# A forgetting-attention and gMLP trunk in split fp32: the input projection's first two column blocks by turns

## The chip, the cores and the metric

The kernel runs on one core of one Trainium2 chip. The metric is device time in microseconds (us), 2053.89 as the median of three runs (2053.75 to 2054.33). Engines are named as in the profile: TensorE is PE (its weight loads PEld), VectorE is DVE, ScalarE is ACT, GpSimd is POOL, and SyncE's queue (SP) issues most transfers.

## The reference

Two layers act on a residual stream of 256 tokens by 2048 channels, in float32. Layer 0 mixes tokens with forgetting attention, layer 1 with a gated MLP over chunks; each is followed by a squared-ReLU MLP. The change lies in the first layer's attention:

```python
h = rmsnorm(x, g_mix[i])
proj = h @ w_in                      # q, k, v (3 x 2048 columns) and 16 gate columns
q = rmsnorm(q, g_q) * HEAD_DIM ** -0.5 ; k = rmsnorm(k, g_k)      # per head of 128
c = cumsum(log_sigmoid(f_logit + b_f))                            # per token and head
s = q @ k.T + (c[t] - c[s]), causal;  o = softmax(s) @ v;  x = x + o @ w_out
x = x + squared_relu(rmsnorm(x, g_mlp[i]) @ w1) @ w2
```

## The kernel before

Every weight is used as two parts, since a product of float32 numbers is made of three on PE: ACT casts a weight to its high part (`split_hi`, L79), DVE subtracts it for the low part (`split_lo`, L87), and PE adds high x high, high x low and low x high (L150 to L152). Weights come in halves of 128 x 1024 numbers (512 KB), called weights below: two blocks of 128 rows by 512 columns each. One **step** is what PE does with one such weight: 2 row blocks x 2 halves of the tokens x 3 products = 12 matmuls of 128 x 512. A column block (512 columns of q, k or v for four heads) takes 8 steps and sums in two PSUM banks (`acc`, one per 128 tokens; four banks in all, so two column blocks at a time). The input projection has 12 column blocks, in the order q, k, v of heads 0 to 3, then q, k, v of heads 4 to 7, and so on; steps 0 to 7 are the first block, 8 to 15 the second.

x transposed lies in DRAM and comes into one buffer (`xT`, named A in the profile) in 8 pieces of 256 KB, two row blocks each. `h_init` scales a piece and splits it in two parts, `H` (ACT L199, DVE L200), and H is then used by every column block.

`run` writes the order of the work by hand. In step i it asks for the weights that are listed for it, splits ahead (low part of step i + 3, high part of step i + 4), issues PE's matmuls, and then the tasks that were put on that step with `at(step, fn)`. All engines take their work in this order. There are 4 buffers for weights, so that the weight of step n + 4 is asked for when the low part of step n has been made; 5 for high parts, 4 for low parts; and two PSUM banks for short use (`aux`).

The tasks around the start are these, with their steps before. `x_norm` (2) asks SP for x itself, 2 MB, and has its squares summed on ACT in step 8 and made into the factor `r_mix` on POOL. `fox_f` (3) asks for the gate's weights, splits them (7), multiplies them with H (9, 16 matmuls) and turns the result to tokens (11); `fox_f_gate` (12) makes the log of the gate and `fox_c` (14) sums it over tokens. `fox_qk` squares a finished q or k block on ACT (L422), takes a power on POOL (L176), one step later scales it on DVE, which frees its accumulator banks (L431), and three steps later transposes it on PE through `aux` (L441). For the first block it is put 3 steps after its last step, 10, for the second at its last step, 15. `fox_bias` (15) fetches the decay rows back from DRAM, `fox_mask` (18) adds the mask; scores come in steps 23 and 24, their transposes in 28 and 29, the outputs in 30 and 31. The second group of heads has its q block done in step 31 and transposed in 34.

## Time and profile before

| | |
|---|---|
| median of three runs | 2053.89 us |
| the profiled execution | 2054.6 us, of which the span is 2052.9 us |
| PE busy | 2045.1 us, 12628 matmul instructions |
| DVE, ACT, POOL busy | 1730.5, 1202.8, 114.4 us |
| HBM read over the span | 430.63 MB, 211 GB/s |

Times inside the profile count from the start of the span. A matmul's busy time is longer than the distance to the next one, as matmuls are pipelined: distances between starts tell whether PE waited. Two instructions in one row, as in "x2", carry their common time.

### The profile page before, as it was taken

To read this page: it belongs to the slowest core of one execution; us is meant where nothing else is said; L and a number is where in the kernel's file an instruction comes from. 1 tells how busy PE (TensorE), PEld (TensorE's weight loads), DVE (VectorE), ACT (ScalarE), POOL (GpSimd) and SP (SyncE) were. 2 spreads that over 40 slices of the span, in tenths; PEclk is the share of its full clock that TensorE was granted. 3 is DMA by queue.
4 is the path that set the end of the run, shared out by engine and by line. 5 is a ranking of instruction groups with operands and counts; after the bars stand their busy time and mean duration, and the time that the engine had idled before them with its cause. 6 is when DMAs were issued, how large, how long until landed. Compare 5 with 4: busy or idle time off the path is not lost.

```text
span 2052.9 us, 32611 instructions
## 1 busy us (share of the span) xinstructions
PE 2045.1 (100%) x12628; PEld 1820.8 (89%) x12628; DVE 1730.5 (84%) x2078; ACT 1202.8 (59%) x1607; POOL 114.4 (6%) x112
## 2 busy tenths in 40 slices
PE   9999999999999999999999999999999999999999
PEld 6888888899999999999988999889999999999997
DVE  5656867779999999999997577768999999999998
ACT  6555555555665656665566455455656556565664
POOL 1110111000000000000000000000000000000000
PEclk9999999999999999999999999999999999999999
DMA  7456666477788877887865567757788777887785
GB/s 278 167 187 209 198 208 204 150 251 226 236 265 270 244 231 234 266 268 232 243 219 190 200 232 212 214 179 235 243 277 249 229 240 257 274 243 228 237 266 166
DMA packets 118602, 469.99 MB, mean 229 GB/s; under 512 B 11808, under 2 KB 30128, under 8 KB 95152
## 3 DMA queue, kind: packets, MB, share of 16 engines
q1 hardware_dynamic: 104352, 395.49, 52.8%
q0 software_dynamic: 13952, 72.37, 19.0%
q8 instruction: 99, 1.62, 0.3%
q14 instruction: 55, 0.45, 0.1%
q10 hardware_dynamic: 144, 0.06, 0.0%
HBM read 430.63 MB, written 2.11 MB: 211 GB/s over the span
## 4 chain that ended last, share of the span: by engine, by line
PE 99%; DMA 1%; ACT 0%; DVE 0%; SPq 0%; issue 0%; DVEq 0%
PE Q L700 14%; PE acc L574 13%; PE acc L575 13%; PE acc L576 13%; PE R L700 10%; PE acc L700 8%; PE acc L150 7%; PE acc L151 7%; PE acc L152 7%; PE acc L763 2%; DMA w_stage<-in_fox_in 1%; PE aux L237 1%; PE aux L899 0%; PE aux L441 0%; PE aux L470 0%; PE aux L519 0%
## 5 line engine op out<-in xcount | busy, mean ns | idle before, releaser
L79 ACT CAST w_hi<-b 128x1024 fp32r<-128x1024 f32 x469 | 486.1, 1048 | 282.7 <-DVE b L729 154.3
L574 PE MATMUL acc<-H,w_hi 128*128 128x256 f32 x2304 | 649.3, 282 | 0.0
L576 PE MATMUL acc<-H,w_lo 128*128 128x256 f32 x2304 | 646.9, 281 | 0.0
L575 PE MATMUL acc<-H,w_hi 128*128 128x256 f32 x2304 | 646.7, 281 | 0.0
L87 DVE TENSOR_TENSOR w_lo<-w_stage,w_hi 128x1024 fp32r<-128x1024 f32 (+1 forms) x470 | 573.0, 1225 | 80.2 <-ACT w_hi L79 38.5
L79 ACT CAST w_hi<-w_stage 128x1024 fp32r<-128x1024 f32 (+1 forms) x470 | 488.6, 1047 | 243.7 <-PE acc L152 80.0
L87 DVE TENSOR_TENSOR w_lo<-b,w_hi 128x1024 fp32r<-128x1024 f32 x469 | 564.5, 1223 | 44.7 <-issue 34.8
L575 PEld LDWEIGHTS acc<-H,w_hi 128*128 128x128 f32 x2304 | 434.1, 188 | 10.4
L574 PEld LDWEIGHTS acc<-H,w_hi 128*128 128x128 f32 x2304 | 433.3, 188 | 10.6
L576 PEld LDWEIGHTS acc<-H,w_lo 128*128 128x128 f32 x2304 | 433.9, 188 | 0.0
L150 PE MATMUL acc<-w_hi,H 128*128 128x512 f32 x512 | 206.4, 403 | 0.4 <-ACT w_hi L79 0.4
L151 PE MATMUL acc<-w_lo,H 128*128 128x512 f32 x512 | 203.4, 397 | 1.4 <-DVE w_lo L87 0.9
L152 PE MATMUL acc<-w_hi,H 128*128 128x512 f32 x512 | 202.9, 396 | 0.0
L700 PE MATMUL Q<-w_hi,SC 128*128 128x512 f32 (+1 forms) x592 | 192.3, 374 | 0.0
L729 DVE TENSOR_TENSOR b<-b,b 128x2048 f32<-128x2048 f32 (+1 forms) x74 | 154.0, 2082 | 0.2
L700 PEld LDWEIGHTS Q<-w_hi,SC 128*128 128x128 f32 x592 | 108.4, 188 | 18.4
L151 PEld LDWEIGHTS acc<-w_lo,H 128*128 128x128 f32 x512 | 96.6, 189 | 24.1 <-DVE w_lo L87 3.1
L152 PEld LDWEIGHTS acc<-w_hi,H 128*128 128x128 f32 x512 | 96.4, 188 | 23.4
L150 PEld LDWEIGHTS acc<-w_hi,H 128*128 128x128 f32 x512 | 96.6, 189 | 22.7 <-ACT w_hi L79 1.2
L700 PE MATMUL Q<-w_lo,SC 128*128 128x512 f32 (+1 forms) x296 | 110.3, 373 | 0.0
L612 ACT ACTIVATE m_a<-m_a 128x512 f32<-128x512 f32 x64 | 40.6, 635 | 114.8 <-DVE m_a L606 113.1
L700 PE MATMUL R<-w_hi,SC 128*128 128x512 f32 (+1 forms) x352 | 107.4, 359 | 0.0
(173 smaller groups left out, 2521.4 us busy)
## 6 DMA issues: line engine op xcount, KB each, us to landing
w_stage<-in_w SPq DMA_DIRECT2D x272, 512.0 KB, 6.5
b<-in_w SPq DMA_DIRECT2D x120, 1024.0 KB, 7.2
w_stage<-in_fox_in SPq DMA_DIRECT2D x94, 512.0 KB, 4.4
b<-in_w POOLq DMA_DIRECT2D x30, 1024.0 KB, 10.6
b<-b POOLq DMA_DIRECT2D x30, 1024.0 KB, 9.2
w_stage<-in_sgu_v SPq DMA_DIRECT2D x32, 512.0 KB, 3.7
w_stage<-in_sgu_u SPq DMA_DIRECT2D x32, 512.0 KB, 5.5
w_stage<-in_sgu_out SPq DMA_DIRECT2D x20, 512.0 KB, 3.9
```

Source lines behind the costliest of these rows:

```text
L79: self.nc.scalar.copy(out=hi[:, sl], in_=self.staged[i][:, sl])
L87: self.nc.vector.tensor_tensor(out=lo[:, sl], in0=st[:, sl], in1=hi[:, sl].bitcast(F32), op=ALU.subtract)
L150: nc.tensor.matmul(out=acc[t], lhsT=xh, rhs=hi[:, ws], start=(kb == k_first), stop=False)
L151: nc.tensor.matmul(out=acc[t], lhsT=xh, rhs=lo[:, ws], start=False, stop=False)
L152: nc.tensor.matmul(out=acc[t], lhsT=xl, rhs=hi[:, ws], start=False, stop=(kb == KB - 1))
L574: nc.tensor.matmul(out=acc[c], lhsT=hi[:, ws], rhs=xh, start=(kb == 0), stop=False)
L575: nc.tensor.matmul(out=acc[c], lhsT=hi[:, ws], rhs=xl, start=False, stop=False)
L576: nc.tensor.matmul(out=acc[c], lhsT=lo[:, ws], rhs=xh, start=False, stop=(kb == KB - 1))
L612: nc.scalar.activation(out=a, in_=a, func=AF.Square)
L700: nc.tensor.matmul(out=bank[bname], lhsT=s, rhs=w[:, ws], start=(before == k == m == 0), stop=(k == 3 and m == 2), skip_group_check=True)
L729: return lambda: nc.vector.tensor_tensor(out=quad[o], in0=quad[x], in1=quad[y], op=op)
L763: nc.tensor.matmul(out=acc[t], lhsT=s, rhs=w[:, ws], start=(q == h == k == m == 0), stop=(q == h == k == 1 and m == 2))
```

## The change

The first two column blocks, q and k of heads 0 to 3, no longer come one after the other but by turns: steps 0, 2, .. 14 are the first block's weights, 1, 3, .. 15 the second's. Each piece of x transposed is then used in two steps. Its transfer is asked for just ahead of the weight of the same step (`load_x`), every second step, where before all eight pieces were asked for at the outset; `h_init` scales it in every second step. The tasks move: `x_norm` to 5 with its squares in 10, `fox_f` to 9 (split 13, product 15, by token 17), the gate to 18, its sums to 21. `fox_qk` of the first block runs in 14, right at its end, that of the second in 20, 5 steps after its end; the decay rows come in 23, the mask in 25, the scores in 27 and 28, their transposes in 32 and 33, the outputs in 34 and 35. From the third block on weights, steps and their tasks stand as before.

```diff
+    def load_x(self, i):
+        if i % 2 == 0 and i < KB:
+            sl = slice(i * S, (i + 2) * S)
+            self.nc.sync.dma_start(out=self.xT[:, sl], in_=self.ins["xT"][:, sl])
+
     def h_init(self, i):
-        for k in (2 * i, 2 * i + 1):
-            self.put_scaled(self.xT[:, k * S:(k + 1) * S], C_GMIX0, k)
+        if i % 2 == 0 and i < KB:
+            for k in (i, i + 1):
+                self.put_scaled(self.xT[:, k * S:(k + 1) * S], C_GMIX0, k)
...
+        two = [self.unit_steps([ins["fox_in"][u * 4 + c] for c in range(4)], "H", done) for u, done in enumerate((
+            lambda acc, step: self.fox_qk(0, 0, acc, step),
+            lambda acc, step: self.at(step + 5, lambda: self.fox_qk(0, 1, acc, step + 5))))]
+        for _ in range(KB // 2):
+            for w in range(2):
+                next(two[w], None)
+                last[0, w] = self.steps - 1
         for g in range(4):
             for w in range(3):
                 u = g * 3 + w
+                if u < 2:
+                    continue
...
-                if u == 0:
-                    last[g, w] = self.unit_x(src, "H", lambda acc, step, done=done: self.at(
-                        step + 3, lambda: done(acc, step + 3)))
-                else:
-                    last[g, w] = self.unit_x(src, "H", done)
-            s = last[g, 1] + (8 if g == 0 else 5)
-            self.at(last[g, 1] + 3, self.fox_mask)
+                last[g, w] = self.unit_x(src, "H", done)
+            s = last[g, 1] + (12 if g == 0 else 5)
+            self.at(last[g, 1] + (10 if g == 0 else 3), self.fox_mask)
...
-        self.at(2, self.x_norm)
-        self.at(9, self.alloc_a)
-        self.at(3, self.fox_f)
-        self.at(12, self.fox_f_gate)
-        self.at(14, self.fox_c)
+        self.at(5, self.x_norm)
+        self.at(KB, self.alloc_a)
+        self.at(9, self.fox_f)
+        self.at(18, self.fox_f_gate)
+        self.at(21, self.fox_c)
...
-        self.at(8, stats)
+        self.at(10, stats)
...
-            self.at(step + (5 if g == 0 else 4), lambda: self.fox_bias(g))
+            self.at(step + (9 if g == 0 else 4), lambda: self.fox_bias(g))
...
-                for i in range(KB // 2):
-                    sl = slice(2 * i * S, 2 * (i + 1) * S)
-                    nc.sync.dma_start(out=xT[:, sl], in_=ins["xT"][:, sl])
-                    if i < STAGE_BUFS:
-                        self.load(i)
+                for i in range(STAGE_BUFS):
+                    self.load_x(i)
+                    self.load(i)
...
                     for j in self.loads.get(i, ()):
+                        self.load_x(j)
                         self.load(j)
-                    if i + SPLIT_AHEAD < KB // 2:
-                        self.h_init(i + SPLIT_AHEAD)
+                    self.h_init(i + SPLIT_AHEAD)
```

SP's queue from the first transfer on, before: A is x transposed, w_stage a weight (the first two in two pieces of 128 x 512), x_res is x.

```order
L990 DMA A<-in_xT 128x512
L65 DMA w_stage<-in_fox_in 128x512 x2
L990 DMA A<-in_xT 128x512
L65 DMA w_stage<-in_fox_in 128x512 x2
L990 DMA A<-in_xT 128x512
L65 DMA w_stage<-in_fox_in 128x1024
L990 DMA A<-in_xT 128x512
L65 DMA w_stage<-in_fox_in 128x1024
L990 DMA A<-in_xT 128x512 x4
L65 DMA w_stage<-in_fox_in 128x1024 x5
L315 DMA x_res<-in_x 128x2048 x2
```

The same place now, from the second transfer on (the first is a piece of x transposed, as before) up to x:

```order
L65 DMA w_stage<-in_fox_in 128x512 x4
L193 DMA A<-in_xT 128x512
L65 DMA w_stage<-in_fox_in 128x1024 x2
L193 DMA A<-in_xT 128x512
L65 DMA w_stage<-in_fox_in 128x1024 x2
L193 DMA A<-in_xT 128x512
L65 DMA w_stage<-in_fox_in 128x1024 x2
L193 DMA A<-in_xT 128x512
L65 DMA w_stage<-in_fox_in 128x1024 x2
L193 DMA A<-in_xT 128x512
L65 DMA w_stage<-in_fox_in 128x1024 x2
L327 DMA x_res<-in_x 128x2048 x2
```

Six pieces of x transposed now stand among twelve weights, and x behind the twelfth weight and not behind the ninth.

PE where the gate's product with H (L342 before, L354 now) stands between two steps, with the waits for other engines, before (steps 9 and 10):

```order
L152 MATMUL acc<-w_hi,H 128x512
L342 MATMUL aux<-H,tt_266 32x512 [waits DVE_49]
L342 MATMUL aux<-H,tt_266 32x512 x15
L150 MATMUL acc<-w_hi,H 128x512
L151 MATMUL acc<-w_lo,H 128x512
L152 MATMUL acc<-w_hi,H 128x512
L150 MATMUL acc<-w_hi,H 128x512
```

and now (steps 15 and 16):

```order
L152 MATMUL acc<-w_hi,H 128x512
L354 MATMUL aux<-H,tt_376 32x512 [waits DVE_49]
L354 MATMUL aux<-H,tt_376 32x512 x15
L150 MATMUL acc<-w_hi,H 128x512 [waits DVE_49,PE_49,Activation_49]
L151 MATMUL acc<-w_lo,H 128x512
L152 MATMUL acc<-w_hi,H 128x512
L150 MATMUL acc<-w_hi,H 128x512 [waits DVE_49,Activation_49]
```

The product has moved to the place where the third block opens its two accumulator banks, each with a wait for DVE.

PE where the first block's q is transposed (L441 before, L453 now), before, at the end of step 13:

```order
L152 MATMUL acc<-w_hi,H 128x512
L441 MATMUL aux<-ident,qk_n 128x128 [waits DVE_49,Activation_49] x2
L441 MATMUL aux<-ident,qk_n 128x128
L441 MATMUL aux<-ident,qk_n 128x128 [waits Activation_49]
L441 MATMUL aux<-ident,qk_n 128x128 [waits DVE_49]
L441 MATMUL aux<-ident,qk_n 128x128 [waits Activation_49]
L441 MATMUL aux<-ident,qk_n 128x128
L441 MATMUL aux<-ident,qk_n 128x128 [waits Activation_49]
L150 MATMUL acc<-w_hi,H 128x512
```

and now, at the end of step 17, with the gate's product by token (L363) ahead of it:

```order
L152 MATMUL acc<-w_hi,H 128x512
L363 MATMUL aux<-sel,probsT 128x16 [waits Activation_49]
L363 MATMUL aux<-sel,probsT 128x16 x3
L453 MATMUL aux<-ident,qk_n 128x128 [waits Pool_49]
L453 MATMUL aux<-ident,qk_n 128x128 x3
L453 MATMUL aux<-ident,qk_n 128x128 [waits Activation_49]
L453 MATMUL aux<-ident,qk_n 128x128 x3
L150 MATMUL acc<-w_hi,H 128x512
```

The fifth transpose opens the second bank of the pair; it waited for DVE before and waits for ACT now.

## Rows read from the trace of the kernel before

**Rows 1.** The page, busy time by engine: us (share of the span) x instructions.

```profile
PE 2045.1 (100%) x12628; PEld 1820.8 (89%) x12628; DVE 1730.5 (84%) x2078; ACT 1202.8 (59%) x1607; POOL 114.4 (6%) x112
```

**Rows 2.** PE's waits over the whole run: who waited for whom, us in total, times, longest.

```profile
PE acc L151 <- DVE w_lo L87: 0.9, 1, 0.9
PE acc L151 <- DVE gq L1010: 0.4, 1, 0.4
```

**Rows 3.** The chain that ended last, from 0 to 40 us: start, us, what.

```profile
9.01 8.70 DMA w_stage<-in_fox_in
17.74 1.05 ACT w_hi L79
...
20.03 1.23 DVE w_lo L87
```

**Rows 4.** PE's timeline: start, us, engine, line, operation; the first matmul of step 1 (10.62), 2 (13.42), 3 (16.84) and 4 (20.00) and what follows, and the gate's products behind step 9.

```profile
8.93 0.63 PE L151 MATMUL acc<-w_lo,H 128*128 128x512 f32 x1
9.36 0.63 PE L152 MATMUL acc<-w_hi,H 128*128 128x512 f32 x1
...
10.62 0.40 PE L150 MATMUL acc<-w_hi,H 128*128 128x512 f32 x1
...
13.42 0.39 PE L150 MATMUL acc<-w_hi,H 128*128 128x512 f32 x1
14.16 0.50 PE L151 MATMUL acc<-w_lo,H 128*128 128x512 f32 x1 [0.35 <-DVE gq L1010]
14.50 0.39 PE L152 MATMUL acc<-w_hi,H 128*128 128x512 f32 x1
...
16.84 0.40 PE L150 MATMUL acc<-w_hi,H 128*128 128x512 f32 x1
17.33 0.50 PE L151 MATMUL acc<-w_lo,H 128*128 128x512 f32 x1
...
20.00 0.39 PE L150 MATMUL acc<-w_hi,H 128*128 128x512 f32 x1
21.31 0.50 PE L151 MATMUL acc<-w_lo,H 128*128 128x512 f32 x1 [0.92 <-DVE w_lo L87]
...
37.97 3.86 PE L342 MATMUL aux<-H,tt 128*32 128x512 f32 x16
41.66 0.39 PE L150 MATMUL acc<-w_hi,H 128*128 128x512 f32 x1
```

**Rows 5.** DVE's timeline: the low parts of the weights of step 0 (two pieces) and step 2.

```profile
5.46 1.33 DVE L87 TENSOR_TENSOR w_lo<-w_stage,w_hi 128x512 fp32r<-128x512 f32 x2
...
12.88 1.22 DVE L87 TENSOR_TENSOR w_lo<-w_stage,w_hi 128x1024 fp32r<-128x1024 f32 x1 [2.62 <-ACT w_hi L79]
```

**Rows 6.** Windows on PE: stretch, its length, PE busy (matmuls), granted clock, share of the transfer engines, GB/s.

```profile
5.00:10.00 5.00, 4.55 (x11) 1.00 0.98 302
10.00:22.00 12.00, 10.64 (x43) 1.00 0.83 322
```

**Rows 7.** Timelines of SP, ACT and DVE: the first weight asked for behind x, its cast and its low part.

```profile
23.24 0.33 SPq L65 DMA_DIRECT2D w_stage<-in_fox_in  x1
...
32.26 1.05 ACT L79 CAST w_hi<-w_stage 128x1024 fp32r<-128x1024 f32 x1 [6.47 <-DMA w_stage<-in_fox_in]
...
33.34 1.23 DVE L87 TENSOR_TENSOR w_lo<-w_stage,w_hi 128x1024 fp32r<-128x1024 f32 x1 [5.17 <-ACT w_hi L79]
```

**Rows 8.** Timelines of PE, ACT, DVE and POOL: the second column block from its last matmul into the first bank (step 15) through the first of its eight squares, the scaled sum, the power and the scaling, to what DVE does next.

```profile
61.12 0.39 PE L152 MATMUL acc<-w_hi,H 128*128 128x512 f32 x1
...
61.61 0.37 ACT L422 ACTIVATE qk_n<-acc,r_mix 128x128 f32<-128x128 f32 x1 [2.42 <-PE acc L152]
...
64.55 0.17 DVE L175 TENSOR_SCALAR r_qk_v<-ss_qk 128x8 f32<-128x8 f32 x1 [3.75 <-ACT qk_n L422]
...
64.87 2.50 POOL L176 TENSOR_TENSOR r_qk<-r_qk_v,mhalf 128x8 f32<-128x8 f32 x1 [4.19 <-DVE r_qk_v L175]
...
67.41 1.41 DVE L431 SCALAR_TENSOR_TENSOR qk_n<-acc,r_mix,r_qk 128x512 f32<-128x512 f32 x2 [1.56 <-POOL r_qk L176]
68.74 2.35 DVE L87 TENSOR_TENSOR w_lo<-w_stage,w_hi 128x1024 fp32r<-128x1024 f32 x2
```

**Rows 9.** Timelines of PE and ACT: the eight transposes of a q block and the two copies of them.

```profile
122.67 1.03 PE L441 MATMUL aux<-ident,qk_n 128*128 128x128 f32 x8
123.31 1.27 ACT L445 ACTIVATE qT<-aux,gq 128x512 f32<-128x512 f32 x2 [2.20 <-PE aux L441]
```

**Rows 10.** Timelines of PE and ACT: the first and last output products of two heads, and the cast of them.

```profile
108.86 0.59 PE L519 MATMUL aux<-probsT,v_nat 128*128 128x256 f32 x2
...
109.94 0.38 PE L521 MATMUL aux<-probsT,v_nat 128*128 128x128 f32 x2
...
110.36 0.59 ACT L204 CAST A<-aux 128x512 fp32r<-128x512 f32 x1 [2.63 <-PE aux L521]
```

**Rows 11.** The instructions that read x (x_res), from 0 to 50 us: count, duration in ns (least, median, most), first and last start.

```profile
L181 ACT ACTIVATE m_a<-x_res x8: 614/614/623, 37.4 to 41.7; 128x512 f32<-128x512 f32 x8
```

**Rows 12.** POOL's timeline of the mask, with its wait for the decay rows, and, from the view of the decay rows in DRAM (one transfer there, four back), the times to landing.

```profile
72.36 1.29 POOL L410 TENSOR_TENSOR tt<-cb,tri 128x512 f32<-128x512 f32 x1 [4.43 <-DMA cb<-c_dram]
73.62 2.27 POOL L411 TENSOR_TENSOR cb<-cb,tri 128x512 f32<-128x512 f32 x1
...
DMA to landing us min/median/max: 3.1/4.8/10.3
```

More of the change, by code (lines that the diff above doesn't have):

```diff
@@ L1004, in run @@
                 for i in range(STAGE_BUFS, LOAD_AHEAD):
+                    self.load_x(i)
                     self.load(i)
```

## The prediction

> **What bounds the kernel now.** I read the page first. TensorE (PE) is busy 2045.1 of 2052.9 us [rows 1], so a change that leaves PE's instructions as they are can move the time only by PE's idle time, and 7.8 us is all there is in the whole span. Next came PE's waits over the whole run: the two releasers of the first 22 us that carry weight are the low part of a weight (0.9 us) and the small `gq` step that stands for it (0.4 us) [rows 2]. The chain that ended last, from 0 to 40 us, tells what is behind them: 8.70 us of a weight transfer asked for at 9.01, then the cast at 17.74, and the subtraction at 20.03 [rows 3]. So the start is bound by the arrival of weights, and from about 22 us on PE is.
>
> How much the start costs is read from when matmuls start, since a busy PE hides short gaps. One step is 12 matmuls; step 1 starts at 10.62 and step 2 at 13.42, so a step without a gap is 2.80 us, 0.233 per matmul [rows 4]. From 10.62 to the products of the forget gate at 37.97 lie steps 1 to 9: 9 x 2.80 = 25.20 if nothing waited, 27.35 as it was. The 2.15 us that were lost are all visible: 13.42 to 14.16 (0.51 too long), 16.84 to 17.33 (0.26), 20.00 to 21.31 (1.08), each followed by one start that comes 0.11 late, as at 14.16 to 14.50 [rows 4]: 0.51 + 0.26 + 1.08 + 3 x 0.11 = 2.18. These are steps 2, 3 and 4, each at its second matmul, the first that reads the low part.
>
> **What the change takes away.** PE has the same instructions in another order, so its own work costs the same. The weights of steps 2, 3 and 4 have fewer bytes ahead of them on SyncE's queue. Up to and with the weight of step 2: before, 3 blocks of x transposed and 3 weights, 2.25 MB; now 2 and 3, 2.0 MB. Step 3: 3.0 against 2.5 MB. Step 4: 4.5 against 3.25 MB. In this stretch the queue moves 302 to 322 GB/s [rows 6], which is 0.8, 1.6 and about 4 us earlier. Needed are 0.45 for step 2 (its low part starts at 12.88, takes 1.22, so ends at 14.10, and the second matmul wants it at 13.65) [rows 4, 5], 0.26 for step 3, 1.08 for step 4. The weight of step 4 also waits for its buffer, which is the first weight's; that one's low part is done at 5.46 + 1.33 = 6.8 [rows 5], so it can be asked for 2.2 us before the 9.01 of rows 3. After that the need falls: two steps take 2 weights and 1 block, 1.25 MB in 5.6 us, or 234 GB/s, under what the queue moves. All three gaps should close. Bounds: 0, if the weights land no earlier, and -2.18; I take -2.18, because the tightest, step 2, has 0.8 where 0.45 is needed.
>
> **What is moved and costs nothing.** x (2 MB) is asked for behind the weight of step 11 and no longer behind that of step 8. What stands behind it on the queue now is the weight of step 12. Before, the weight asked for at 23.24, just behind x, was cast at 32.26 after 6.47 us of waiting, and its low part was ready at 34.57 for step 9 at about 35.2, with 0.6 to spare [rows 7]. With the same 9 us, step 12's lands near 32 and is wanted at 10.62 + 11 x 2.80 = 41.4. The squares of x, 8 of 0.61 us on ScalarE [rows 11], stand in step 10 and not 8, the first user of their result in step 14; ScalarE is through with them near 42 and with the casts behind them by 48, and step 14 ends at 49.8. If that cover went, ScalarE's lateness would be paid in full at the next point. The decay rows go to DRAM in step 21 and come back for the mask; ahead of that the gap was six steps and is now four. One such transfer lands 3.1 us after its issue at the least, the way back waited 4.4 us, and the mask takes 1.29 + 2.27 us [rows 12]: about 12 us from the end of step 21 (77 us by my count) gives 90; the scores of step 27 come near 95. Nothing.
>
> **What it adds: the first block's banks.** Both column blocks now hold the four accumulator banks until step 15, and step 16 opens the third block in the first one's banks. The order of PE between steps 15 and 16 (shown with the change) has two L150 that wait for VectorE: that is the scaling by the norm, which frees the two banks. Behind them stand all further matmuls. How long that takes is in the trace at step 15 of before, the same work on the second block: its first bank is whole with the matmul at 61.12, the squares run from 61.61, the sum is scaled at 64.55, GpSimd's power takes 2.50 from 64.87, and the scaling is done between 67.41 and 68.74 [rows 8]. The matmul at 61.12 is the tenth of its step, so the step ends at 61.12 + 4 x 0.233 = 62.05: first bank free 6.0 us after it (half of 1.41 after 67.41), the second 6.7. Cover: step 15 (2.80) and the 16 products between (41.66 - 37.97 = 3.69 [rows 4]) make 6.49, and the second bank is wanted 0.70 later. It just fits, with 0.4 us. Bounds: 0, and some 4.9 us if all the squares of x [rows 11] still stood ahead on ScalarE; I take 0, the nearer.
>
> **What it adds: two waits for a small bank.** There are two auxiliary banks. In step 17 the gate's product by token and the transposes of q now stand together, and the gate is read in step 18 only. In PE's order at the end of step 17 (shown with the change) the fifth transpose waits for ScalarE, as the gate's values keep one bank and the second four transposes must take the bank of the first four. In the kernel before the product by token stood two steps ahead of them. The price is in the transposes of 122.67: ScalarE's copy starts 0.64 after the first transpose, two copies take 1.27 [rows 9], so the bank is free at 0.64 + 0.64 = 1.28, and PE would want it after 4 transposes, at 1.03 / 8 x 4 less overlap, or 0.4. That is a wait of 0.9. The same kind comes in step 34: the attention output of the first heads is put 4 steps later, from step 30 to 34, where the transposes of the next q block stand. Output and transposes need three banks. The output products start at 108.86, the last at 109.94, and ScalarE's cast of them at 110.36 [rows 10]; a cast is about 0.5, then the copy of the first transposes 0.64: free 2.65 us after 108.86, wanted at 1.22 + 0.40 = 1.62. That is 1.05. Bounds for both together: 0 (another bank is free after all) to 2.8 (VectorE's part of the output is waited for each time); I take 0.9 + 1.05 = 1.95.
>
> **Sum.** -2.18 + 0 + 0 + 1.95 = -0.23 us, on the profiled execution's own 2054.6 us (its span and 1.7 around it). That execution is 0.7 above the median of the runs, 2053.89; on the median it makes 2053.7 us.
>
> **A rule against the start.** The first step's matmuls start 0.43 us apart (8.93 to 9.36) and from 10.62 on 0.233 [rows 4]; 0.43 for 512 columns is the 1.2 GHz level, though the granted clock reads 1.00 from 5 us on [rows 6]. The change puts nothing other there. The Trainium skill (TensorE: Matmul & The Clock Gate, The HAM clock gate) says that the unit which grants the clock runs freely, and so the rise does not come at a fixed matmul of a kernel. By that rule the time could move by itself; the three times of before lie within 0.6 us, which speaks against much of it. It is the last rival below.
>
> **Rivals.**
> 1. The gaps close and the two bank waits cost nothing, as ScalarE may be quicker or another bank free: -2.18, 2051.7. For it: the copies are short. Against it: the wait on ScalarE stands in the order.
> 2. The gaps stay: the weights land no earlier because all transfers share the queue's time, and only the new waits are seen: 2053.9 + 1.95 = 2055.8. For it: the queue moved 302 to 322 GB/s while PE waited [rows 6]. Against it: 1.25 MB fewer are ahead of step 4's weight.
> 3. Slower: the first block's banks in step 16. From 0.4 us of lateness on, each further us on ScalarE, VectorE or GpSimd is paid by PE. With the squares of x in the way, 4.9 - 0.4 = 4.5: 2053.7 + 4.5 = 2058.2.
> 4. The rise of the clock falls elsewhere: ten matmuls of the first step at 0.43 instead of 0.233 are 2.0 us, so 2051.7 or 2055.7.
>
> **How the numbers follow.** Forecast 62%, own range 2052.9 to 2054.7 (half a us on either term); rival 1 12%, rival 2 10%, rival 3 11% (half of it small, 1 to 2 us), rival 4 5%. The range reaches over rival 1 and 2 and the small part of 3: 2051.4 to 2056.4. A change of 0.2%, 4.1 us, is about what a measurement of this kernel can tell from none. Faster by that is out of reach of the 2.18 us the start can give; it is left 3%. Slower by it needs the larger part of rival 3 or a wait that I have not seen: 6%. The rest, 91%, is no change.
>
> **What would show it.** In the profile of the changed kernel: from step 1 on to the products (now ahead of step 16) starts lie 0.233 apart, 15 x 2.80 = 42.0 us, so the products start near 52.6. No low part is waited for by the second matmul of steps 2 to 4. After the products L150 follows in 3.7 us; more is rival 3. In steps 17 and 34 the four transposes and the next four lie about 1.3 us apart at their starts and not 0.4. Wrong would be any PE wait beyond these before 130 us, or a first block of weights that lands as late as before.

## The result and the profile after

| | before | changed |
|---|---|---|
| median, 17 runs each | 2053.81 us (2053.47 to 2054.50) | 2057.91 us (2056.14 to 2061.58) |
| profiled execution, its span | 2054.6, 2052.9 us | 2057.55, 2055.8 us |

The ratio is 1.0021, 95% interval 1.0014 to 1.0028: the changed kernel is slower, by 4.1 us, and 1.5 us above the forecast range. The page's first part, against [rows 1]:

```profile
PE 2044.5 (99%) x12628; PEld 1820.5 (89%) x12628; DVE 1729.6 (84%) x2078; ACT 1203.2 (59%) x1607; POOL 114.3 (6%) x112
```

PE did the same work in 0.6 us less busy time, so the 2.9 us that the span grew are idle time. PE's waits over the whole run, against [rows 2] (us in total, times, longest):

```profile
PE acc L150 <- DVE qk_n L443: 2.4, 1, 2.4
PE aux L453 <- ACT qT L457: 1.6, 2, 0.8
...
PE acc L151 <- DVE w_lo L87: 0.6, 2, 0.3
```

The two waits of the start are nearly gone. One new wait of 2.4 us stands at the top: the scaling of q, which frees the first block's banks. The second row is the two expected waits for a small bank. These are idle times; by the distances between starts, used from here on, the first is 2.53 us and the second 2.04. PE's timeline of that place, against [rows 4]:

```profile
8.98 0.40 PE L150 MATMUL acc<-w_hi,H 128*128 128x512 f32 x1
...
45.38 0.39 PE L150 MATMUL acc<-w_hi,H 128*128 128x512 f32 x1
46.09 0.50 PE L151 MATMUL acc<-w_lo,H 128*128 128x512 f32 x1 [0.33 <-DVE w_lo L87]
...
51.56 3.86 PE L354 MATMUL aux<-H,tt 128*32 128x512 f32 x16
57.78 0.47 PE L150 MATMUL acc<-w_hi,H 128*128 128x512 f32 x1 [2.37 <-DVE qk_n L443]
...
59.06 0.63 PE L152 MATMUL acc<-w_hi,H 128*128 128x512 f32 x1
59.49 0.63 PE L150 MATMUL acc<-w_hi,H 128*128 128x512 f32 x1
...
62.05 0.55 PE L150 MATMUL acc<-w_hi,H 128*128 128x512 f32 x1
62.43 0.40 PE L151 MATMUL acc<-w_lo,H 128*128 128x512 f32 x1
```

Step 1 starts at 8.98, step 14 at 45.38, the gate's products at 51.56. In step 14 the second and third matmul come 0.59 later than at 0.233 a start, for a late low part. The products want 3.69 us [rows 4], so step 16 could have begun at 55.25; it began at 57.78, 2.53 late. Then, from 59.06 on, the starts lie 0.43 apart, the 1.2 GHz level, and come back to 0.233 at 62.43. The windows on PE show the fall in the granted clock too (columns as in [rows 6]):

```profile
60.00:62.00 2.00, 2.00 (x6) 0.50 0.65 213
62.00:64.00 2.00, 2.00 (x9) 0.91 0.12 49
```

Added over its matmuls, that stretch costs 1.57 us. The chain that ended last, from 28 to 58 us, leads back from the late bank (columns as in [rows 3]):

```profile
28.73 8.76 DMA w_stage<-in_fox_in
37.59 1.05 ACT w_hi L79
...
46.10 3.93 DMA w_stage<-in_fox_in
51.08 1.78 ACT qk_n L434 x10
54.27 2.60 POOL r_qk L176
56.89 0.76 DVE qk_n L443
57.78 0.47 PE acc L150
```

The squares of q began at 51.08. What stood ahead of them is in the timelines of ScalarE, which answers to the cast of [rows 7] and the squares of [rows 11], and of VectorE:

```profile
34.40 1.05 ACT L79 CAST w_hi<-w_stage 128x1024 fp32r<-128x1024 f32 x1 [5.87 <-PE acc L152]
...
37.59 1.05 ACT L79 CAST w_hi<-w_stage 128x1024 fp32r<-128x1024 f32 x1 [0.39 <-DMA w_stage<-in_fox_in]
38.55 0.63 ACT L181 ACTIVATE m_a<-x_res 128x512 f32<-128x512 f32 x1
...
43.47 0.89 ACT L206 ACTIVATE H<-A,par 128x256 fp32r<-128x256 f32 x2
44.26 2.93 ACT L79 CAST w_hi<-w_stage 128x1024 fp32r<-128x1024 f32 x3
...
50.13 1.05 ACT L79 CAST w_hi<-w_stage 128x1024 fp32r<-128x1024 f32 x1 [2.63 <-DMA w_stage<-in_fox_in]
51.08 0.36 ACT L434 ACTIVATE qk_n<-acc,r_mix 128x128 f32<-128x128 f32 x1
```

```profile
43.59 0.16 DVE L186 TENSOR_REDUCE tot_mix<-ss_mix 128x2 f32<-128x8 f32 x1 [4.55 <-ACT m_a L181]
...
43.99 0.91 DVE L207 SCALAR_TENSOR_TENSOR H<-A,par,H 128x256 fp32r<-128x256 f32 x2
44.83 3.48 DVE L87 TENSOR_TENSOR w_lo<-w_stage,w_hi 128x1024 fp32r<-128x1024 f32 x3
```

The first row names PE, but PE had long been done with that buffer; it is the weight of step 12, asked for at 24.47 behind x's 2 MB, that came late. ScalarE stood idle from 28.5 to 34.4 for it, and from then to 47.5 for 0.39 us only. The squares of x ran from 38.55 to 43.5, the last pieces of H stood behind them, and behind H, on VectorE, the low part of step 14, the first of the three from 44.83 on. That low part frees the buffer of the weight of step 18: asked for at 46.10, landed at 50.0, cast at 50.13. That cast stands in ScalarE's order ahead of the squares of q, which by the pattern of [rows 8] would have begun 0.44 us before the end of step 14, at 48.76 (51.56 less a step) - 0.44 = 48.32. They came 2.76 late. Of this the forecast's 0.4 us of margin is covered, and 2.36 are paid; from the squares to step 16 it then took 6.70 us, about 0.2 more than [rows 8] gave, which makes up the wait of 2.53.

An account of the profiles in the same way tells where the time went. "Start" is the products' start against 54.77, which is the 37.97 of before and six steps more (where they follow step 14, 51.97); "stretch" what matmuls at the 1.2 GHz level behind a stop cost; "small banks" what the transposes of steps 17 and 34 wait.

| us against before | start | wait at step 16 | stretch | small banks | sum | span, measured |
|---|---|---|---|---|---|---|
| changed | -3.21 | 2.53 | 1.57 | 2.04 | +2.93 | +2.9 |
| again | -2.15 | 2.49 | 1.66 | 2.04 | +4.04 | +4.0 |
| stats7 | -2.30 | 0 | 0 | 2.05 | -0.25 | -0.3 |
| x_spread | -3.49 | 2.45 | 0 | 2.04 | +1.00 | +0.9 |
| nopause | -3.18 | 2.49 | 0 | 0 | -0.69 | -0.6 |
| lockstep | -1.71 | 0 | 0 | 0 | -1.71 | -1.7 |
| mended2 | -2.47 | 0 | 0 | 0 | -2.47 | -2.5 |

The names are those of the experiments below. Four terms make up every span of the table to 0.1 us.

How often the stretch comes is told by the granted clock that each execution reports, to three places. In the 15 profiled executions it reads 0.999 in the six that show a stretch behind a stop and 1.000 in the nine that show none. Of the changed kernel's 17 executions the five fastest read 1.000 (2056.14 to 2057.35 us), the next nine 0.999 (2057.55 to 2059.69) and the three slowest 0.998 (2060.17 to 2061.58). By this reading most of its spread goes with the clock, and most executions had a stretch, some more than one. The reading is rounded: 4 of 85 executions of the kernel before, timed beside the experiments, read 0.999 too and lie among the rest (2053.54 to 2054.39).

### The profile page after: what moved, and what is told of

The parts are those of the page before. It is cut to its first block, busy times and chain, and to the rows that moved or that the text cites. A ratio compares the mean times of both kernels' runs of the same rounds, so it can differ in the third digit from the quotient of the medians.

```text
span 2055.8 us, 32606 instructions
## 1 busy us (share of the span) xinstructions
PE 2044.5 (99%) x12628; PEld 1820.5 (89%) x12628; DVE 1729.6 (84%) x2078; ACT 1203.2 (59%) x1607; POOL 114.3 (6%) x112
## 4 chain that ended last, share of the span: by engine, by line
PE 98%; DMA 1%; ACT 1%; issue 0%; POOL 0%; DVE 0%; DVEq 0%; ACTq 0%; SPq 0%
PE Q L712 14%; PE acc L586 13%; PE acc L587 13%; PE acc L588 13%; PE R L712 10%; PE acc L712 8%; PE acc L150 7%; PE acc L151 7%; PE acc L152 7%; PE acc L775 2%; DMA w_stage<-in_fox_in 1%; PE aux L244 1%; PE aux L453 0%; PE aux L911 0%; PE aux L482 0%; PE aux L531 0%
```

## The experiments

The theory was the chain above: ScalarE, late by the squares of x, holds the bank. The rivals were that the landing of the weights behind x does it, whatever ScalarE has to do, that the sum of the squares on VectorE does it, and that much of the loss is the clock's and not the wait's. A run without an interval is one execution beside the kernel before.

**again.** The changed kernel as it is, to see what repeats.

> The changed kernel once more, nothing edited. Theory A (a chain on ScalarE makes PE wait ahead of step 16, and the clock falls after that wait): the wait between the gate's products and step 16 is there again, 2 to 3 us beyond the products' own 3.7 us, and matmuls behind it start 0.43 us apart for a while, but the length of that stretch and of the slow one at the start (0 to 12 matmuls) may differ, since the runs spread over 5.4 us. Rival B (the wait is chance, as a late transfer): the wait changes by more than 1 us or is gone.

2058.57 us. The wait at step 16 came again, 2.49, and so did the small banks; step 1 started 1.5 us later, at 10.49. The stretch at 1.2 GHz was not behind step 16 but behind the pause in step 17, from 67.41 to 70.8:

```profile
67.00 0.66 PE L453 MATMUL aux<-ident,qk_n 128*128 128x128 f32 x4 [0.78 <-ACT qT L457]
67.41 0.58 PE L150 MATMUL acc<-w_hi,H 128*128 128x512 f32 x1
67.79 0.63 PE L151 MATMUL acc<-w_lo,H 128*128 128x512 f32 x1
68.22 0.63 PE L152 MATMUL acc<-w_hi,H 128*128 128x512 f32 x1
```

The wait came again at its full length; the place of the stretch and the start changed.

**stats7.** The squares of x three steps earlier.

```diff
-        self.at(10, stats)
+        self.at(7, stats)
```

> Only edit: the squares of x run in step 7 and no longer in step 10. Theory A1 (the squares stand in step 10 behind a cast that waits for its weight, so all that ScalarE does later is late by their 4.9 us, down to the squares of the first block's q): they fill ScalarE's idle time of 28.5 to 34.4 us, the weight of step 18 is asked for some 4 us earlier than 46.1, the first square of q starts within 0.5 us of the last matmul that it needs and no longer 2.8 us late, the wait ahead of step 16 is under 0.5 us, the clock doesn't fall there: 2053 to 2054.5 us against 2057.9. Rival A2 (the power, the sum and the scaling of the first block take too long by themselves): the wait stays at 2 us or more, 2057 us.

2053.65 us (2052.85 to 2055.15), ratio 0.9999 (0.9990 to 1.0009). ScalarE and PE in its timelines:

```profile
30.45 0.63 ACT L181 ACTIVATE m_a<-x_res 128x512 f32<-128x512 f32 x1 [1.36 <-DMA x_res<-in_x]
...
35.50 1.04 ACT L79 CAST w_hi<-w_stage 128x1024 fp32r<-128x1024 f32 x1
...
47.35 1.05 ACT L79 CAST w_hi<-w_stage 128x1024 fp32r<-128x1024 f32 x1 [0.43 <-DMA w_stage<-in_fox_in]
...
49.22 0.37 ACT L434 ACTIVATE qk_n<-acc,r_mix 128x128 f32<-128x128 f32 x1 [0.82 <-PE acc L152]
```

```profile
52.47 3.85 PE L354 MATMUL aux<-H,tt 128*32 128x512 f32 x16
56.16 0.40 PE L150 MATMUL acc<-w_hi,H 128*128 128x512 f32 x1
```

The squares run as soon as x has landed, in the time in which ScalarE had stood idle for the weight; the weight of step 18 was asked for at 42.18 instead of 46.10 and cast at 47.35; the squares of q now wait for PE; step 16 follows the products in 3.69. The weight of step 12 was cast at 35.50, no earlier than in the changed kernel (34.40), so its late landing does not by itself hold the bank. One number moved, and the kernel does what was forecast for the change, with the two small banks still there.

**x_spread.** x in four pieces of 512 KB, each behind the weight of a step, so that no weight has 2 MB ahead of it.

```diff
-        self.at(5, self.x_norm)
+        self.at(4, self.x_norm)
...
-        for t in range(NT):
-            nc.sync.dma_start(out=self.x[:, t, :], in_=self.ins["x"][:, t * D:(t + 1) * D])
...
+        part(0)
+        for j in range(1, 4):
+            self.at(self.now + j, lambda j=j: part(j))
```

> Only edit: x is asked for in four pieces of 512 KB behind the weights of steps 10, 11, 12 and 13 and no longer in two of 1 MB behind that of step 11; the squares stay in step 10. Theory A1: ScalarE is late because the weights of steps 12 to 14 arrive late behind x (cast of step 12's at 34.4 when its turn was 28.6). With smaller pieces between them that weight is cast by 32, the squares begin 1 to 3 us earlier than 38.55, and the wait ahead of step 16 falls by as much, from 2.5 to about 0 to 1.5: 2054 to 2057 us. If the total of the transfers is the limit and not their order, the weight of step 14 lands as late as before and nothing is gained: 2057.9.

2056.75 us (2055.49 to 2059.97), ratio 1.0017 (1.0007 to 1.0026). The late landing of step 12's weight is gone (cast at 31.47), and the wait at step 16 is not (2.45):

```profile
31.47 1.05 ACT L79 CAST w_hi<-w_stage 128x1024 fp32r<-128x1024 f32 x1 [2.10 <-PE acc L151]
...
37.30 1.05 ACT L79 CAST w_hi<-w_stage 128x1024 fp32r<-128x1024 f32 x1 [2.21 <-PE acc L152]
38.26 0.63 ACT L181 ACTIVATE m_a<-x_res 128x512 f32<-128x512 f32 x1
```

The squares stand in line behind step 14's cast, and start at 38.26 as against 38.55. The second row names PE, but by its starts PE was done with step 9, whose high part had that buffer, at 34.3: what came late is the weight, asked for at 28.39, where the changed kernel asked at 28.73 and cast at 37.59. So this edit moved the late landing from step 12's weight to step 14's, as the second half of the expectation had it, and does not tell what an early landing of all weights would give. With the squares where they are, asking for x in pieces does not help.

**sum_late.** Only the sum of the squares, on VectorE and GpSimd, two steps later.

```diff
-            self.total_rsqrt(ss, "mix0")
+            self.at(12, lambda: self.total_rsqrt(ss, "mix0"))
```

> Only edit: the sum of x's squares and its power are put into step 12 and no longer right behind the squares in step 10. Theory A1a (VectorE is held by that sum, so that the low part of step 14's weight is late, its buffer free late, and the weight of step 18 asked for late): VectorE goes on by 38 us, the weight of step 18 is asked for 4 us earlier, the wait ahead of step 16 is gone. Theory A1b (the low part of step 14 stands behind the scaling of x transposed's last piece, which stands behind the squares on ScalarE itself): the low part still starts near 44.8, the wait stays within 0.3 us of the 2.5 us.

2057.32 us, with a wait of 2.56. The low part of step 14 started at 44.59 and not 44.83. VectorE's sum is not what held it by more than that 0.24. What is left ahead of it on VectorE is its share of H, which waited for ScalarE.

**half.** Four squares of x instead of eight (this leaves half of the numbers out of the norm's sum).

```diff
-                for n in range(4):
+                for n in range(2):
...
-            self.total_rsqrt(ss, "mix0")
+            self.total_rsqrt(ss[:, :, 0:2], "mix0")
```

> Leaves out half of x's squares (4 of 8, so the norm's factor is too large); all else, and their place in step 10, as in the changed kernel. Theory A1 (ScalarE has no idle time from 34.4 to 47.5 us, and what is put into that stretch is paid behind it): 4 x 0.615 = 2.46 us less there, the weight of step 18 is asked for 2.4 us earlier, the squares of q start 2.4 us earlier, the wait ahead of step 16 falls from 2.5 to 0 to 0.3 us. Rival A3 (the place of the squares matters and not their length, as they hold VectorE or the weights' queue): the wait stays above 1.5 us.

2053.64 us. The wait fell from 2.53 to 0.67; the 0 to 0.3 expected left out that the products would start 0.50 earlier too, at 51.06, as step 14 no longer waits for its low part. Step 18's weight was asked for at 43.59 instead of 46.10, cast at 47.77, and the squares of q ran at once behind it:

```profile
47.77 1.05 ACT L79 CAST w_hi<-w_stage 128x1024 fp32r<-128x1024 f32 x1 [2.77 <-PE acc L152]
48.73 0.36 ACT L434 ACTIVATE qk_n<-acc,r_mix 128x128 f32<-128x128 f32 x1
```

Taking 2.4 us of squares off ScalarE brought the request forward by 2.5 and the squares of q by 2.35. Each link of the chain moved by that amount.

**stats8.** The squares of x in step 8.

```diff
-        self.at(10, stats)
+        self.at(8, stats)
```

> Only edit: the squares of x in step 8 and not in step 10. In that order they still stand behind the cast of step 12's weight, for which ScalarE waits until 34.4. Theory A1: the same work in the same full stretch in another order, so the wait ahead of step 16 stays at 2.0 to 2.6 us, and the casts of steps 13 and 14 come later, with a gap of some tenths in those steps. Rival (each step earlier helps by a step's share): two thirds of what step 7 gave, wait under 1 us.

2058.35 us. The wait ahead of step 16 went (0.06), and the loss came 15 us earlier, in steps 12 and 13:

```profile
40.98 0.39 PE L152 MATMUL acc<-w_hi,H 128*128 128x512 f32 x1
41.83 0.49 PE L150 MATMUL acc<-w_hi,H 128*128 128x512 f32 x1 [0.46 <-ACT H L206]
...
43.89 0.80 PE L151 MATMUL acc<-w_lo,H 128*128 128x512 f32 x1 [1.56 <-DVE w_lo L87]
44.48 0.63 PE L152 MATMUL acc<-w_hi,H 128*128 128x512 f32 x1
```

0.62, 1.83 and 0.36 longer than 0.233, 2.8 in all, and a stretch at 1.2 GHz behind them, of 1.2 more. This is one execution. I had expected a smaller loss at the old place. In step 8 the squares stand behind the cast of the late weight (35.42) and ahead of the H of step 12, which came at 41.29 and which PE waits for in the second row. So what counts is not earlier or later: in step 7 they stand ahead of the late weight's cast, in ScalarE's idle time.

**nopause.** The forget gate one step earlier (8, 17, 19) and the next tasks two, so that no two of these stand in steps 17 and 34 together; the squares of x stay in step 10.

```diff
-            s = last[g, 1] + (12 if g == 0 else 5)
-            self.at(last[g, 1] + (10 if g == 0 else 3), self.fox_mask)
+            s = last[g, 1] + (10 if g == 0 else 5)
+            self.at(last[g, 1] + (8 if g == 0 else 3), self.fox_mask)
...
-        self.at(9, self.fox_f)
-        self.at(18, self.fox_f_gate)
-        self.at(21, self.fox_c)
+        self.at(8, self.fox_f)
+        self.at(17, self.fox_f_gate)
+        self.at(19, self.fox_c)
...
-            self.at(step + (9 if g == 0 else 4), lambda: self.fox_bias(g))
+            self.at(step + (7 if g == 0 else 4), lambda: self.fox_bias(g))
```

> The kernel mended, but with the squares of x in step 10 as in the changed kernel: the wait ahead of step 16 is there, the two bank waits of steps 17 and 34 are not. Theory A1: the wait ahead of step 16 is 2.3 to 2.6 us (now right ahead of step 16, as the gate's products stand a step earlier). Under C1 the clock still falls behind it in some runs: 2054.5 to 2056.5, spread over 3 us. Under C2 most of the falls are gone with the pause in step 17: 2053.8 to 2054.8, spread under 2.5 us. The kernel with the squares in step 7 has 2052.5, so what lies above that is the wait and what the clock does behind it.

2054.95 us (2053.01 to 2057.36), ratio 1.0006 (0.9996 to 1.0016). The wait is still there, between 55.06 and 57.78 (2.49), the transposes wait no more, and the profile has no stretch at 1.2 GHz. But of the ten executions the five slowest, from 2055.41 on, read a granted clock of 0.999, and the five others, the profiled one among them, 1.000. By that reading the clock falls in half of the executions though step 17 has no pause, as theory C1 had it.

**mended.** Both edits: the squares in step 7 as in stats7, and the tasks as in nopause.

```diff
-        self.at(10, stats)
+        self.at(7, stats)
...
-        self.at(9, self.fox_f)
+        self.at(8, self.fox_f)
```

> The changed kernel with the squares of x in step 7, and the two waits for a small bank taken out: the gate's products in step 14, by token in 16, read in 17 ahead of the transposes; decay sums in 19, the rows fetched in 21, mask 23, scores 25 and 26, outputs 32 and 33, so that they no longer meet the transposes of step 34. Theory G (the three waits are all that the change costs): no wait ahead of step 16, transposes of steps 17 and 34 without a pause between the fourth and fifth, 2.05 us under the kernel with the squares in step 7 (2053.65): 2051.6, and 2.2 under before. Rival: the mask comes too late for the scores of step 25, and TensorE waits there 1 us or more: 2052.5 to 2054.

2052.50 us (2050.70 to 2052.96), ratio 0.9991 (0.9982 to 1.0000). No wait at step 16, none in 17 and 34, but 0.9 above the 2051.6 of theory G. A new gap of 1.67 us in step 11: the sum of the squares, which waits for ScalarE, now holds the low part behind it on VectorE:

```profile
37.72 0.16 DVE L186 TENSOR_REDUCE tot_mix<-ss_mix 128x2 f32<-128x8 f32 x1 [7.56 <-ACT m_a L181]
37.99 1.23 DVE L87 TENSOR_TENSOR w_lo<-w_stage,w_hi 128x1024 fp32r<-128x1024 f32 x1
```

These four kernels differ in two edits only, so their medians make a square (they were not all timed on one chip, but the kernel before lay between 2053.81 and 2054.00 beside each):

| median us | small banks waited for | not waited for |
|---|---|---|
| wait at step 16 | 2057.91 (changed) | 2054.95 (nopause) |
| no wait | 2053.65 (stats7) | 2052.50 (mended) |

Without the small banks the wait is worth 2.45, and without the wait the small banks are worth 1.15; both together are worth 5.41, 1.81 more than the two. These are not clean prices. mended has its new gap of 1.67, which the three others lack, and the 2.45 holds the stretches of half of nopause's executions. That 1.81 is about one stretch at 1.2 GHz, but drawing the executions of the four kernels anew gives anything from -0.8 to 3.2 (95%), so the square does not show that the wait and the pauses make each other dearer.

**fill.** Is it the 16 thin products (32 columns of weights) ahead of the wait that let the clock fall? Eleven more of them ahead, in the time of the wait.

```diff
-            for kb in range(KB):
+            for kb in range(-11, KB):
```

> Only edit: 11 products of the gate are made once more ahead of the 16, so that TensorE works through the 2.5 us in which it waits for the bank (they add 11 x 0.233 = 2.56 us of work and nothing to the result). Theory C (the wait costs its 2.5 us, and the rest of the loss is the clock, which falls after the wait in some runs and not in others): step 16 starts at the same time as in the changed kernel, no matmul behind it starts 0.43 us apart, 2055.5 to 2056.5 us and no run above 2058, against 2057.9 and 2061.6. Rival D (the rest of the loss has another cause, as transfers or the two bank waits): 2057.5 to 2058.5, spread as before; if the wait isn't covered but added to, 2060.

2057.88 us (2057.06 to 2059.77), ratio 1.0020 (1.0011 to 1.0029). The wait was filled, 53.53 to 59.74 without a stop, and the clock fell behind the pause in step 17 (68.56 to 71.93, about 1.6 us). The time is that of rival D and the cause that of theory C, at another stop, so this does not decide.

**fill128.** The same with eleven full matmuls of 128 x 512 behind the products, their result unused.

```diff
+            pf = self.aux()
+            for kb in range(11):
+                nc.tensor.matmul(out=pf, lhsT=self.H[:, kb, 0, 0:P], rhs=self.H[:, kb, :, :].rearrange("p a s -> p (a s)"),
+                                 start=True, stop=True)
```

> The changed kernel with 11 full matmuls (128 x 128 by 512, result unused) behind the gate's products, to fill the wait ahead of step 16; the earlier filler was 32 columns wide. Theory C1 (in the runs above 2056 the clock falls behind the unfilled wait ahead of step 16; a filler as wide as the steps' matmuls keeps it up): step 16 starts as in the changed kernel, no slow stretch behind it, nor behind step 17; 2055.5 to 2056.5, no run above 2058. Rival C2 (the clock falls behind the pause in step 17 just as well, whatever was done ahead of step 16): slow stretches behind 67 us in some runs, 2056.5 to 2058.

2058.40 us (2056.93 to 2060.61), ratio 1.0022 (1.0012 to 1.0031). The clock did not fall behind step 16, and fell again behind the pause in step 17:

```profile
63.87 0.66 PE L457 MATMUL aux<-ident,qk_n 128*128 128x128 f32 x4
65.31 0.66 PE L457 MATMUL aux<-ident,qk_n 128*128 128x128 f32 x4 [0.78 <-ACT qT L461]
...
66.41 0.63 PE L152 MATMUL acc<-w_hi,H 128*128 128x512 f32 x1
66.84 0.63 PE L150 MATMUL acc<-w_hi,H 128*128 128x512 f32 x1
```

In this profile work of PE's own in the wait's place kept the clock up there, and it fell at the next stop, at 1.6 us. So keeping PE busy through the wait gained nothing.

**lockstep.** From the other side: the kernel before, one block after the other, with only its transfers changed: each piece of x transposed is asked for just ahead of a weight, not all at the outset.

```diff
+    def load_x(self, i):
+        if i < KB // 2:
+            sl = slice(2 * i * S, 2 * (i + 1) * S)
+            self.nc.sync.dma_start(out=self.xT[:, sl], in_=self.ins["xT"][:, sl])
...
+                for i in range(STAGE_BUFS):
+                    self.load_x(i)
+                    self.load(i)
```

> The kernel before with one part of the change alone: the pieces of x transposed are asked for one by one ahead of the weight of the same step, the first two column blocks one after the other as before. The weight of step 4 then has 3.75 MB up to and with it, where it had 4.5 before and 3.25 in the changed kernel. Theory S (bytes ahead on the queue set the start): the gaps of steps 2 to 4 shrink from 2.18 us to 0.5 to 1.2, but a step then wants 768 KB in 2.8 us, 281 GB/s, near what the queue moves, and x itself comes in among them, so that some of it comes back by step 9: 2052.5 to 2054 us. Rival (turns are needed for any gain): within 0.3 us of 2053.8.

2052.86 us (2052.38 to 2053.17), ratio 0.9994 (0.9985 to 1.0004); each of its 10 runs lies below the lowest of the kernel before in that comparison, 2053.54. The products start at 36.26 instead of 37.97: most of the start's gaps close without turns.

**before_cold.** The kernel before with one warming matmul at the outset instead of four, to see what the clock at the start costs there.

```diff
-                for i in range(4):
+                for i in range(1):
```

> The kernel before with 1 warming matmul at the start and not 4, so that TensorE's first steps run at half speed for longer. Theory E (in the kernel before the start is paced by the arrival of the weights, so what the clock does in the first steps is absorbed in the gaps of steps 2 to 4): more slow matmuls in steps 0 to 1, smaller gaps in 2 to 4, the weight of step 4 lands near 17.7 us as before, time within 0.7 us of 2053.8. Rival F (the clock's rise moves the end one for one): 1.5 us and more above.

2053.81 us (2053.61 to 2054.25), ratio 0.9999 (0.9990 to 1.0008). Step 1 started at 10.29, a little earlier, and the gap in step 4 was 1.46 instead of 1.08:

```profile
19.27 0.39 PE L150 MATMUL acc<-w_hi,H 128*128 128x512 f32 x1
20.96 0.50 PE L151 MATMUL acc<-w_lo,H 128*128 128x512 f32 x1 [1.31 <-DVE w_lo L87]
```

The products started at 37.63 instead of 37.97. That is by as much as the weight of step 4 landed earlier, 17.38 instead of 17.71: it is the weight that sets the products' start here. PE reached step 4 by 0.73 earlier (19.27 for 20.00) and kept no more than the weight's 0.34. The matmuls at the 1.2 GHz level did not become more (5 instead of 8), so this says little on warming.

**mended2.** mended, with the sum of the squares put in step 10, to take the new gap away.

```diff
-            self.total_rsqrt(ss, "mix0")
+            self.at(10, lambda: self.total_rsqrt(ss, "mix0"))
```

> The kernel mended (squares in step 7, the two bank waits taken out), and the sum of the squares with its power in step 10, so that VectorE isn't held by it while it should make the low part of step 11's weight: mended waited 1.67 us for that at 37.37. Theory H: that gap goes, no other wait from step 1 on but tenths; 2050.7 to 2051.7 us, against 2052.5 of mended, and with less spread, since nothing is left behind which the clock could fall. Rival: the gap comes from x landing at 32.5, and ScalarE's squares then make the next cast late by themselves: 2052.0 to 2052.6.

2052.48 us (2050.85 to 2053.49), ratio 0.9993 (0.9984 to 1.0002). The gap is gone and the median stays; why is not shown. The profiled execution is 0.8 shorter than that of mended, although its step 1 began 1.24 later (10.30 for 9.06). It beats the changed kernel by 5.4 us and lies 1.3 below the kernel before, which its interval does not quite tell from no difference.

## Why the prediction was wrong

- **The start, -2.18: right.** The three gaps closed. stats7, whose start is nearest to the one of before (step 1 at 10.47), gave -2.30. In the changed kernel's own profile it is -3.21: step 1 began 1.64 us earlier there, and 0.59 went again in step 14, at a wait for a low part that the forecast did not have (half and stats7 are without it).
- **The two small banks, 0.9 + 1.05: right.** 1.02 each, by the mechanism that was forecast.
- **The squares of x, "Nothing", and the first block's banks, "I take 0, the nearer": wrong, and here the prediction failed.** They were one term. Its bounds, 0 and 4.9, held the measured 2.53; the value taken did not. The times I gave ScalarE were near (through with the squares at 43.5 for 42, with the casts behind them at 47.2 for 48). What I left out was the next link: the low part of step 14 stands behind the squares, its buffer takes the weight of step 18, and the cast of that weight stands ahead of the squares of q. I compared the end of ScalarE's work with the end of step 14, and did not follow what that work makes late for a second pass through the queue. It was rival 3, at 2.5 us for its 4.5. (The matmul at 61.12 in [rows 8] is the ninth of its step, not the tenth; the step's end worked out from it, 62.05, is right.)
- **No price for the clock behind a stop: missed.** Rival 4 put the clock at the start alone. Of the 4.3 us between the medians of the changed kernel and stats7, 2.5 are the wait. The 1.8 that are left are near the 1.6 of the stretch at 1.2 GHz in both profiles of the changed kernel, and 12 of its 17 executions read a granted clock under 1.000 against 1 of 10 of stats7.
- **Rival 4, the clock at the start: partly right.** It neither made nor broke the result, but it is in the spread. The changed kernel began step 1 at 8.98, with no start 0.43 apart ahead of it, and the same kernel at 10.49 in again, with six. Over all profiles of the kernels by turns it lies between 8.96 and 10.91 us. Before, the weights pace the start (before_cold), and 17 executions lie within 1.0 us; by turns, PE paces itself, and where the clock seldom falls later the ends lie 2.3 us apart (stats7, mended). The changed kernel's 5.4 us hold the later stretches as well. The rule weighed there (the Trainium skill, TensorE: Matmul & The Clock Gate, The HAM clock gate), that the rise is tied to no fixed matmul of a kernel, agrees with the two starts of the same kernel, 8.98 and 10.49.
- **Rivals 1 and 2:** both fell, as the banks were waited for and the gaps closed.

## What to carry to other kernels

Where work moves into a stretch, follow it through the in-order queues for a second round: what it delays, which buffer that frees late, and which transfer's cast then stands ahead of the operation on the critical path. Work that is to be hidden belongs into an idle time that the trace shows on its engine (here ScalarE's wait for a weight behind 2 MB, step 7), since one step later (stats8) or three (the changed kernel) it was paid at another place. And try the transfers' order by itself first: it gave most of the start's gain here without any of the moves that lost it.

## What the runs showed of the hardware

Behind a stop of 2.5 us, or of about 1 us among small products, the clock may fall to 1.2 GHz for some 3 us, which costs 1.5 to 1.7 us again. Profiles show it in the changed kernel, again, sum_late, fill, fill128 and stats8, in each behind one of its stops only, and not in x_spread, whose stops were the same as the changed kernel's. Nor did it come behind the stops in step 4 of before and before_cold (1.08 and 1.46 us) or in step 11 of mended (1.67). By the granted clock that each execution reports:

| kernel | stops | executions under 1.000 |
|---|---|---|
| changed | wait at step 16, small banks | 12 of 17 |
| x_spread | the same | 5 of 10 |
| nopause | wait at step 16 | 5 of 10 |
| fill, fill128 | wait filled, small banks | 7 and 8 of 10 |
| stats7 | small banks | 1 of 10 |
| lockstep, mended, mended2 | neither | 0 of 10, 11 and 11 |
| before | neither | 4 of 85 |

So the wait can bring a fall without the pauses, the pauses alone hardly did, and filling the wait did not prevent it. What decides whether and where it comes stays open. And a granted clock of 1.00 in a window does not exclude such a stretch: in [rows 6] it reads 1.00 for the 5 us in which [rows 4] shows starts 0.43 apart. The distance between starts is the surer sign.
